# One forget-bias tile per head, and new task costs and transfer model in the planner of a hybrid-attention layer

## The chip, the cores and the metric

The kernel runs on one core of one Trainium2 chip. The metric is the device time of one execution in microseconds; the median over several executions is given. A profiled execution has a time of its own. Engines are called as in the profile: PE (matrix), PEld (its weight loads), DVE (vector), ACT (scalar), POOL (GpSimd) and SP, which here only issues DMAs.

## What is computed

One layer of a streaming encoder, for a prompt of 16 + 1024 rows and, with the same weights, for 32 new rows behind 272 cached ones. Each row of 1024 is normalised (RMSNorm) and projected by one weight into queries, keys and values of two attention groups, 8 forget logits and a gate of 1024 columns. The two groups are four differential heads with a distance bias and eight forgetting heads with a bias from summed log forget gates. Their outputs are concatenated, multiplied by SiLU of the gate, projected by a second weight, added to the input and normalised. New keys, values and log gates are outputs too. Of the reference, the forgetting heads are the part that the change touches:

```python
F = jnp.cumsum(LF, axis=1)
sf = jnp.einsum('bqhe,bkhe->bhqk', qf, Kf).astype(f32) * scale
sf = sf + (Fq_t[:, :, :, None] - Fk_t[:, :, None, :])
sf = jnp.where(kidx[None, :] <= qidx[:, None], sf, NEG)
pf = jax.nn.softmax(sf, axis=-1)
of = jnp.einsum('bhqk,bkhe->bqhe', pf.astype(Vf.dtype), Vf)
```

As the softmax takes out whatever is the same for a whole row, the kernel adds only F of the key minus a constant.

## The kernel before, in words

Everything is written as tasks: an engine, an estimated cost in ns, a function that emits the instructions, a priority (lower comes first), the tasks it depends on and the buffers that it takes and gives back. `Graph.order` (L149) plays the tasks through in time: each engine, when free, takes the ready task of the lowest priority number whose buffers can be had. The order in which tasks begin there is the order in which the instructions are written, and each engine, SP too, runs its own in that order. So the costs, which are set by hand at each `add`, decide the order, but not how long anything takes on the chip. A result is taken to reach another engine after 300 to 500 ns (`HOPS`, L33). Costs come from formulas by columns (`c_mm`, `c_act`, `c_dve`, `c_ts`, `c_pool`, from L266) or from a number. A DMA task holds SP for 480 ns (`dma`, L281), a transpose for 1190; its transfer is played as `moved`, in `order`, which adds 650 ns before, 2.85 ns for each KB and 900 ns behind, with eight in flight at most.

Buffers are rings of so many tiles (`RINGS`) and an `arena` in which room is sought for each use. Rings are counted, but the tile framework hands out a ring's tiles in turn.

The stages of work: the inputs are normalised and transposed into `hT` (`x_tasks`). For each of 8 pairs `p` of columns, `w_tasks` (L611) loads 512 KB of weight into `raw` (L625), takes the largest absolute value on ACT (L627), spreads it over the partitions by a diagonal on POOL (L583) and a matmul on PE (L587), and rounds the weight into two halves of 16 bits; `proj_tasks` multiplies (L827). Pairs 0 to 3 are the differential heads, pairs 4 to 7 two forgetting heads each. `pair_tasks` then makes the attention units: a unit (`unit_tasks`, L1206) is one head with two blocks of 128 queries, `gg` from 0 to 3; for the forgetting pairs head 0 and head 1 take turns for each `gg`. In a unit PE writes scores into one of two PSUM banks `sc` (L1235), DVE adds the bias tile and takes the minimum in one pass (L1249), ACT takes the exponential (L1255), DVE, ACT and POOL split the probabilities into two halves, SP transposes them by DMA from `arena` to `arena` (L1335), and PE multiplies by the values (L1347 to L1349 differential, L1351 and L1352 forgetting). Later pairs' projections and the gates' have high priority numbers and fill PE in between. `out_tasks` (L1607) loads the mixed columns and the gate of one tile of rows (L1719, L1720), multiplies, takes the largest absolute value (L1737), rounds (L1740 on ACT, L1742 on DVE), multiplies by the output weight (L1770), adds the input (L1784) and normalises (L1808), and stores (L1811).

The bias of the forgetting heads: `forget_tasks` makes F for all 8 heads and 1040 rows on 8 partitions, subtracts from it one of four constants (its value at row 16 + 256 `gg`, L1113) and stores the four versions to `G_s` in DRAM. For each pair, `bias_tasks` (L1148) loads its 8 rows (L1177), scales them on POOL (L1180) and stores them to `G_t` (L1184). For each unit it then fetches the first 272 + 256 `gg` columns of one row, broadcast to all 128 partitions, into a tile of the ring `G`, which has two (L1192):

```python
n = 272 + 256 * gg
sp.dma_start(out=loc["t"][:, :n], in_=G_t.rearrange("h n -> (h n)")[None, 8320 * (p - 4) + c:8320 * (p - 4) + c + n]
             .broadcast_to([128, n]))
```

The ring `G` also holds the distance tile of the differential pairs and, at either end, the gains of the two norms.

## Time and profile before

| | |
|---|---|
| time, median of 3 runs (lowest to highest) | 882.83 us (881.67 to 883.38) |
| the profiled execution: its time, its span | 879.12 us, 877.4 us |
| mean granted PE clock of the span | 0.909 |
| busy: PE, DVE, ACT, POOL | 80%, 72%, 57%, 47% |
| DMA: moved in the span, share of the 16 engines of the hardware queue | 119.27 MB, 60.4% |

A busy share is the time in which an engine has an instruction under way. The rest is waiting, and lists of waits say what ended it. A matmul's record also holds its way through the array, so that PE's instructions overlap and a busy PE can still be short of its peak. The clock is given as a share of 2.4 GHz.

### The profile page before, as it was taken

To read this page: it belongs to the slowest core of one execution; us is meant where nothing else is said; L and a number is where in the kernel's file an instruction comes from. 1 tells how busy PE (TensorE), PEld (TensorE's weight loads), DVE (VectorE), ACT (ScalarE), POOL (GpSimd) and SP (SyncE) were. 2 spreads that over 40 slices of the span, in tenths; PEclk is the share of its full clock that TensorE was granted. 3 is DMA by queue.
4 is the path that set the end of the run, shared out by engine and by line. 5 is a ranking of instruction groups with operands and counts; after the bars stand their busy time and mean duration, and the time that the engine had idled before them with its cause. 6 is when DMAs were issued, how large, how long until landed. Compare 5 with 4: busy or idle time off the path is not lost. (4 is left out here: it accounts for less than half of the span.)

```text
span 877.4 us, 14974 instructions
## 1 busy us (share of the span) xinstructions
PE 703.1 (80%) x4967; PEld 456.3 (52%) x4967; DVE 633.0 (72%) x1672; ACT 496.5 (57%) x1136; POOL 414.3 (47%) x602
## 2 busy tenths in 40 slices
PE   4578887987876999899796978689788962888776
PEld 4455554665544576566564755356556542233333
DVE  5976587877766887988985857497797895454443
ACT  5843574666553776676675665377568752242222
POOL 2575233977556866866743654445452244200000
PEclk7679989999998999999998989799999985698899
DMA  8672426454423554554499688467959989753511
GB/s 248 122 147 62 93 54 88 106 94 103 95 65 74 127 102 98 115 117 115 105 194 182 127 168 163 111 144 167 208 123 204 277 204 243 232 173 121 153 63 49
DMA packets 240558, 119.27 MB, mean 136 GB/s; under 512 B 150569, under 2 KB 229745, under 8 KB 240481
## 3 DMA queue, kind: packets, MB, share of 16 engines
q1 hardware_dynamic: 240480, 118.32, 60.4%
q8 instruction: 39, 0.64, 0.3%
q14 instruction: 39, 0.31, 0.1%
HBM read 57.18 MB, written 22.07 MB: 90 GB/s over the span
## 5 line engine op out<-in xcount | busy, mean ns | idle before, releaser
L827 PE MATMUL pj<-hT,Whi 128*128 128x384 f16 (+4 forms) x1328 | 314.7, 321 | 2.0 <-DVE ge L938 1.5
L827 PE MATMUL pj<-hT,Wlo 128*128 128x416 f16 (+4 forms) x664 | 212.6, 320 | 4.4 <-DVE Wlo L648 4.4
L827 PEld LDWEIGHTS <-Whi 128*128 128x128 f16 x1328 | 133.3, 102 | 78.5 <-issue 11.5
L1249 DVE CUSTOM_DVE_ANT_0 arena<-sc,G,stats 128x400 f32<-128x400 f32 (+6 forms) x224 | 129.9, 590 | 43.3 <-PE sc L1235 22.4
L1255 ACT ACTIVATE arena<-arena,stats 128x144 f32<-128x144 f32 (+7 forms) x128 | 99.9, 780 | 38.8 <-DVE stats L1249 31.6
L1235 PE MATMUL sc<-k,q 128*128 128x400 f16 (+6 forms) x448 | 97.1, 317 | 29.4 <-DVE stats L1249 25.7
L583 POOL TENSOR_SCALAR diag<-ident,stats 128x128 bf16<-128x128 f32 x51 | 26.1, 513 | 154.9 <-ACT Wlo L1737 68.5
L827 PEld LDWEIGHTS <-Wlo 128*128 128x128 f16 x664 | 67.6, 102 | 38.1 <-DVE Wlo L648 4.7
L1351 PE MATMUL av<-arena,vn 128*128 128x128 f16 x288 | 43.9, 236 | 45.2 <-DMA arena<-arena 44.7
L1235 PEld LDWEIGHTS <-q 128*128 128x128 f16 x448 | 40.8, 101 | 57.6 <-issue 41.1
L627 ACT ACTIVATE Wlo<-raw 128x1024 bf16<-128x1024 f32 x27 | 28.5, 1055 | 63.8 <-DMA raw<-in_w_in_dram 63.8
L1770 PEld LDWEIGHTS <-Whi 128*128 128x128 f16 (+2 forms) x304 | 30.1, 102 | 58.7 <-issue 16.5
L827 PE MATMUL pj<-hT,Wghi 128*128 128x256 f16 (+2 forms) x240 | 58.2, 326 | 0.0
L1770 PE MATMUL pj<-arena,Whi 128*128 128x512 f16 (+4 forms) x152 | 49.7, 413 | 9.8 <-ACT Whi L1740 7.1
L1352 PEld LDWEIGHTS <-vn 128*128 128x128 f16 x288 | 30.7, 107 | 48.6 <-issue 47.6
L1290 POOL TENSOR_TENSOR arena<-arena 128x16 f16<-128x16 f32 (+7 forms) x56 | 46.5, 853 | 12.4 <-ACT arena L1284 12.1
L1306 DVE SCALAR_TENSOR_TENSOR arena<-arena,stats 128x128 f16<-128x128 f32 (+4 forms) x80 | 49.6, 663 | 2.6 <-ACT arena L1298 2.4
L1323 POOL TENSOR_TENSOR arena<-arena 128x16 f16<-128x16 f32 (+3 forms) x48 | 36.0, 773 | 25.8 <-ACT arena L1317 25.7
L1789 ACT ACTIVATE arena<-arena 128x512 bf16<-128x512 f32 (+3 forms) x19 | 11.5, 603 | 61.4 <-DVE arena L1784 61.4
L1352 PE MATMUL av<-arena,vn 128*128 128x128 f16 x288 | 44.3, 237 | 0.0
L1784 DVE SCALAR_TENSOR_TENSOR arena<-pj,stats,arena 128x512 f32<-128x512 f32 (+3 forms) x19 | 13.7, 721 | 42.3 <-PE pj L1770 38.9
L587 PE MATMUL tr<-diag,onesb 128*128 128x128 bf16 x51 | 11.7, 229 | 36.9 <-POOL diag L583 24.6
(310 smaller groups left out, 1786.7 us busy)
## 6 DMA issues: line engine op xcount, KB each, us to landing
raw<-in_w_in_dram SPq DMA_DIRECT2D x32, 512.0 KB, 7.5
arena<-in_x_prompt_dram SPq DMA_DIRECT2D x16, 512.0 KB, 9.7
raw<-in_w_out_dram SPq DMA_DIRECT2D x16, 512.0 KB, 4.6
k<-k SPq DMA_DIRECT2D x16, 268.0 KB, 3.4
G<-G_t SPq DMA_DIRECT2D x8, 520.0 KB, 4.7
mix_s<-mx SPq DMA_DIRECT2D x32, 128.0 KB, 3.4
arena<-mix_s SPq DMA_DIRECT2D x8, 512.0 KB, 6.3
arena<-gate_s SPq DMA_DIRECT2D x8, 512.0 KB, 6.0
```

The lines of the kernel that those rows point to most:

```text
L583: pool.tensor_scalar(out=loc["d"], in0=ident, scalar1=col_, scalar2=1.0, op0=ALU.mult, op1=ALU.mult)
L627: ta = add("act", c_act(1024), lambda: act.activation(out=loc["lo"].bitcast(BF16), in_=loc["raw"], func=AF.Abs, accum_out=a), prio, [tl], ...
L827: mm(out, (W["hi"], W["hi"], W["lo"])[w][:, k, :], (hTh, hTl, hTh)[w][:, k, c0:c1], start=i == 0, stop=i == 23)
L1235: mm(s[:, :b - a], q, K[p]["t"][:, m, x, a:b], start=x == 0, stop=x == 1 and not mask)
L1249: dve.tensor_tensor_reduce(out=A(ph, nk)[:, a:b], in0=loc["s"][:, :b - a], in1=bl["t"][:, o + a:o + b], scale=Q[p]["tau"], scalar=3e38 if ...
L1255: te = add("act", c_act(nk) + 150, lambda ph=ph, nk=nk, mn=mn, sm=sm: act.activation(out=A(ph, nk), in_=A(ph, nk), func=AF.Exp, scale=-1.0 ...
L1290: (pool if on_pool else dve).tensor_tensor(out=A16(w, o, o + b - a), in0=x[:, a:b], in1=A16(w, h, h + b - a), op=ALU.subtract)
L1306: dve.scalar_tensor_tensor(out=A16(w, o, o + b - a), in0=x[:, a:b], scalar=rk, in1=A16(w, h, h + b - a), op0=ALU.mult, op1=ALU.subtract)
L1323: pool.tensor_tensor(out=A16(w, o, o + b - a), in0=x[:, a:b], in1=A16(w, h, h + b - a), op=ALU.subtract)
L1351: mm(out, vn[:, j, 128 * hd:128 * hd + 128], hi, start=j == 0, stop=False)
L1352: mm(out, vn[:, j, 128 * hd:128 * hd + 128], lw, start=False, stop=False)
L1770: mm(d, a, b, start=k == 0 and i == 0, stop=k == 7 and i == len(ops) - 1)
```

## The change

It has two parts. First, the forget bias: F is taken against one constant only (its value at row 528), stored once per head, scaled once, and fetched once per head of a pair, with all 1040 columns, by one broadcast. Both heads' tiles stay in the ring `G` until their last unit. Second, the planner: nearly every cost is set to another number, a matmul is taken to be slower for a while behind a long pause (`COLD`), the time for a result to reach another engine depends on the engine that gives it (`HOPS`), rings are handed out in turn, and transfers follow one another: a plain DMA's data begins when the one before is through, and a transpose holds SP from shortly before that until its own cost is over and lands 2000 ns later. A part of the output projection is taken to hold only the two weights that it reads.

```diff
-HOPS = [400.0, 300.0], [500.0, 300.0]
+HOPS = {"pe": 220.0, "sp": 100.0, "act": 80.0, "dve": 80.0, "pool": 80.0}
+SLACK = {"pe": 0.0, "act": 0.0, "dve": 0.0, "pool": 0.0, "sp": 0.0}
+COLD = 3400.0
+TRANSPOSED = 2000.0
+LANDED = 1600.0
...
-MARGIN = 1.1
...
-                if self.free[h.ring] < 1:
+                if self.slots[h.ring][self.turn[h.ring]]:
                     break
-                self.free[h.ring] -= 1
+                h.at = self.turn[h.ring]
+                self.slots[h.ring][h.at] = True
+                self.turn[h.ring] = (h.at + 1) % self.free[h.ring]
...
-                    d.ready = max(d.ready, now + (0.0 if d.eng == t.eng else HOPS[d.eng == "pe"][d.prio > 10400]))
+                    d.ready = max(d.ready, now + (0.0 if d.eng == t.eng else HOPS[t.eng] + SLACK[d.eng]))
...
-                        busy[e] = now + t.cost
+                        cost = t.cost
+                        if e == "pe":
+                            if now > last + COLD:
+                                slow = COLD
+                            cost += min(cost, slow)
+                            slow = max(0.0, slow - cost + t.cost)
+                            last = now + cost
+                        busy[e] = now + cost
                         done = busy[e]
-                        if e == "sp":
-                            moved = max(done + 650.0, moved) + t.move
-                            done = moved + 900.0
-                            flight = (flight + [done] * t.n)[-8:]
-                            if len(flight) == 8:
-                                busy[e] = max(busy[e], flight[0])
+                        if t.dma:
+                            if t.block:
+                                busy[e] = done = moved = max(now, moved - 300.0) + t.cost
+                                done += TRANSPOSED
+                            else:
+                                busy[e] = max(busy[e], moved - 4000.0)
+                                moved = max(busy[e] + 300.0, moved) + t.move
+                                done = moved + LANDED
...
-        return k * max(107.0, 0.417 * n)
+        return k * max(56.0, 2.5 + 0.417 * n)
     def c_act(n, k=1):
-        return MARGIN * k * (75.0 + 0.84 * n)
+        return k * (165.0 + 0.85 * n)
     def c_dve(n, k=1):
-        return MARGIN * k * (65.0 + 1.05 * n)
+        return k * (165.0 + 1.08 * n)
     def c_ts(n):
-        return MARGIN * (100.0 + 1.1 * n)
+        return 240.0 + 1.05 * n
     def c_pool(n, k=1):
-        return MARGIN * k * (100.0 + 2.2 * n)
-    def dma(fn, prio, deps=(), acq=(), use=(), kb=128, n=1, spare=(), cost=480.0):
-        t = add("sp", cost * n, fn, prio, deps, acq, use, 2.85 * kb, spare)
+        return k * (160.0 + 2.2 * n)
+    def dma(fn, prio, deps=(), acq=(), use=(), kb=128, n=1, spare=(), cost=440.0, move=4.5, block=False):
+        t = add("sp", cost * n, fn, prio, deps, acq, use, move * kb, spare)
         t.n = n
+        t.dma = True
+        t.block = block
...
-    G_s = dr.tile([NH, 4 * 1040], F32, tag="G_s", name="G_s")
-    G_t = dr.tile([NH, 4 * 1040], F32, tag="G_t", name="G_t")
+    G_s = dr.tile([NH, 1040], F32, tag="G_s", name="G_s")
+    G_t = dr.tile([NH, 1040], F32, tag="G_t", name="G_t")
...
-        t1 = add("act", cost + 330, f1, prio, deps, [], use)
-        return r, t1, add("dve", 530, f2, prio, [t1, by and by[1]])
+        t1 = add("act", cost + 420, f1, prio, deps, [], use)
+        return r, t1, add("dve", 1170, f2, prio, [t1, by and by[1]])
...
-                    kb=5 * w, cost=1190.0)
+                    kb=5 * w, cost=2640.0, block=True)
...
-        td = add("pool", 260, fd, prio, list(deps) + [cn["id"]], [dh])
-        return loc, th, add("pe", 110, f, prio, [td, cn["one"]], [th], [dh])
+        td = add("pool", 370, fd, prio, list(deps) + [cn["id"]], [dh])
+        return loc, th, add("pe", 60, f, prio, [td, cn["one"]], [th], [dh])
...
-        tl = dma(fl, prio, [], [rh, wh], kb=512)
+        tl = dma(fl, prio, [], [rh, wh], kb=512, move=10.0)
...
-        t4 = add("pool", 1500, f4, prio, [t3], [], [sh, vh])
+        t4 = add("pool", 3000, f4, prio, [t3], [], [sh, vh])
...
-        for gg in range(4):
-            n = 1040
-            gh = Hold("arena", n)
-            def fg(gg=gg, n=n, gh=gh):
-                F = A(Fh, 1040, NH)
-                b = 16 + 256 * gg
-                dve.tensor_scalar(out=A(gh, n, NH), in0=F[:, :n], scalar1=F[:, b:b + 1], scalar2=None, op0=ALU.subtract)
-            tg = add("dve", 65 + 0.6 * n, fg, prio, carry, [gh], [Fh])
-            G_done[gg] = dma(lambda gg=gg, n=n, gh=gh: sp.dma_start(
-                out=G_s[:, 1040 * gg:1040 * gg + n], in_=A(gh, n, NH)), prio, [tg], [], [gh])
+        gh = Hold("arena", 1040)
+        def fg():
+            F = A(Fh, 1040, NH)
+            dve.tensor_scalar(out=A(gh, 1040, NH), in0=F, scalar1=F[:, 528:529], scalar2=None, op0=ALU.subtract)
+        tg = add("dve", 65 + 0.6 * 1040, fg, prio, carry, [gh], [Fh])
+        G_done["p"] = dma(lambda: sp.dma_start(out=G_s, in_=A(gh, 1040, NH)), prio, [tg], [], [gh])
...
-    def bias_tasks(p, hd, gg, prio, G_done):
+    def bias_tasks(p, hd, prio, G_done):
...
-        n = 272 + 256 * gg
-        if ("G", p) not in samp:
+        if hd == 0:
             gh = Hold("arena", 1040)
             a = 2 * (p - 4)
             def fl():
-                sp.dma_start(out=A(gh, 1040, 8), in_=G_s[a:a + 2].rearrange("h (g n) -> (h g) n", g=4))
+                sp.dma_start(out=A(gh, 1040, 2), in_=G_s[a:a + 2])
             def fm():
-                pool.tensor_scalar(out=A(gh, 1040, 8), in0=A(gh, 1040, 8), scalar1=Q[p]["inv"][:8], scalar2=1.0,
+                pool.tensor_scalar(out=A(gh, 1040, 2), in0=A(gh, 1040, 2), scalar1=Q[p]["inv"][:2], scalar2=1.0,
                                    op0=ALU.mult, op1=ALU.mult)
             def fo():
-                sp.dma_start(out=G_t[a:a + 2].rearrange("h (g n) -> (h g) n", g=4), in_=A(gh, 1040, 8))
-            t = dma(fl, prio - 50, [G_done[x] for x in range(4)] + [Q[p]["t_tau"]], [gh], kb=33)
+                sp.dma_start(out=G_t[a:a + 2], in_=A(gh, 1040, 2))
+            t = dma(fl, prio - 50, [G_done["p"], Q[p]["t_tau"]], [gh], kb=8)
             t = add("pool", 100 + 1.1 * 1040, fm, prio - 50, [t], [], [gh])
-            samp["G", p] = dma(fo, prio - 50, [t], [], [gh], kb=33)
+            samp["G", p] = dma(fo, prio - 50, [t], [], [gh], kb=8)
+        c = 2 * (p - 4) + hd
         def f():
             loc["t"] = T([128, 1040], F32, "G", RINGS["G"])
-            c = 1040 * (4 * hd + gg)
-            sp.dma_start(out=loc["t"][:, :n], in_=G_t.rearrange("h n -> (h n)")[None, 8320 * (p - 4) + c:8320 * (p - 4) + c + n]
-                         .broadcast_to([128, n]))
-        cn["bias"] = dma(f, prio, [samp["G", p], cn["bias"]], [h], kb=n / 2)
+            sp.dma_start(out=loc["t"], in_=G_t[c:c + 1].broadcast_to([128, 1040]))
+        cn["bias"] = dma(f, prio, [samp["G", p], cn["bias"]], [h], kb=520)
...
-                     prio, [tl], [z], [w], kb=20 * nt, cost=1190.0)
+                     prio, [tl], [z], [w], kb=20 * nt, cost=1100.0 + 40.0 * nt, block=True)
...
-                             [ph] if part == 0 else [], [wh] + wholds + ([ph] if part else []))
+                             [ph] if part == 0 else [], [wh] + wholds[2 * part:2 * part + 2] + ([ph] if part else []))
...
-        dist = None
+        dist = {}
         for u, (hd, gg) in enumerate(units):
-            if p >= 4 or u == 0:
-                dist = bias_tasks(p, hd, gg, base + u - 1, G_done)
+            if hd not in dist:
+                dist[hd] = bias_tasks(p, hd, base + u - 1, G_done)
             if hd == 0:
                 av = {}
-            unit_tasks(p, hd, gg, base + u, dist, av)
+            unit_tasks(p, hd, gg, base + u, dist[hd], av)
```

Left out are further costs of single tasks, changed in the same way, among them those of the sample rows' tasks and of the rounding in the units.

## Rows read from the trace of the kernel before

**Rows 1.** Head of the page: the span.

```profile
span 877.4 us, 14974 instructions
PE 703.1 (80%) x4967; PEld 456.3 (52%) x4967; DVE 633.0 (72%) x1672; ACT 496.5 (57%) x1136; POOL 414.3 (47%) x602
```

**Rows 2.** Busy by stage: stretch, its length, each engine's busy us (instructions), clock, DMA.

```profile
100.00:360.00 260.00, 221.81 (x1621) 148.34 (x1619) 199.94 (x552) 160.49 (x380) 167.56 (x225) 0.95 0.46 92
360.00:720.00 360.00, 300.04 (x2391) 207.35 (x2391) 282.55 (x810) 238.73 (x550) 178.92 (x285) 0.96 0.76 162
720.00:877.00 157.00, 114.12 (x513) 50.49 (x512) 76.81 (x161) 42.70 (x95) 20.10 (x21) 0.82 0.51 148
```

**Rows 3.** PE's waits, whole span: who waited for whom, us, times, longest.

```profile
PE av L1351 <- DMA arena<-arena: 44.7, 21, 8.7
PE sc L1235 <- DVE stats L1249: 25.7, 29, 3.0
PE tr L587 <- POOL diag L583: 24.6, 9, 5.6
...
PE tr L587 <- ACT stg L712: 8.7, 3, 5.9
...
PE av L1347 <- DMA arena<-arena: 1.8, 2, 1.1
```

**Rows 4.** Line L1335, 100 to 370 us: ns on SP (min/median/max), then landing.

```profile
L1335 SPq DMA_TRANSPOSE arena<-arena x25: 1177/1401/5860, 109.6 to 366.1; - x25
...
DMA to landing us min/median/max: 2.6/3.8/5.8
```

**Rows 5.** The same line, 370 to 740 us.

```profile
L1335 SPq DMA_TRANSPOSE arena<-arena x71: 1177/1760/6361, 371.9 to 731.2; - x71
...
DMA to landing us min/median/max: 3.3/4.6/13.0
```

**Rows 6.** Timeline of SP, 545 to 554 us: start, us, what.

```profile
545.69 1.03 SPq L625 DMA_DIRECT2D raw<-in_w_in_dram  x1
546.89 6.36 SPq L1335 DMA_TRANSPOSE arena<-arena  x1
```

**Rows 7.** DMA queue and issues, 370 to 735 us: KB each, median us to landing.

```profile
q1 hardware_dynamic: 129574, 59.36, 76.2%
...
raw<-in_w_in_dram SPq DMA_DIRECT2D x12, 512.0 KB, 7.4
G<-G_t SPq DMA_DIRECT2D x8, 520.0 KB, 4.7
...
G<-G_t SPq DMA_DIRECT2D x8, 136.0 KB, 3.4
```

**Rows 8.** Longest waits of all engines, whole span.

```profile
ACT Wlo L627 <- DMA raw<-in_w_in_dram: 63.8, 21, 8.2
```

**Rows 9.** Line L1192: ns on SP (min/median/max), first and last start.

```profile
L1192 SPq DMA_DIRECT2D G<-G_t x32: 319/392/1590, 371.0 to 701.4; - x32
```

**Rows 10.** Line L1113, the subtractions of the forget task.

```profile
L1113 DVE TENSOR_SCALAR arena<-arena x4: 743/744/749, 133.7 to 135.7; 8x1040 f32<-8x1040 f32 x4
```

**Rows 11.** PE's waits, 720 to 878 us.

```profile
PE pj L1770 <- ACT Whi L1740: 7.1, 4, 1.9
PE pj L1770 <- DVE Wlo L1742: 6.9, 4, 2.8
PE tr L587 <- POOL diag L583: 5.6, 1, 5.6
PE tr L587 <- DVE stats L600: 3.4, 4, 1.0
PE pj L1770 <- DVE Whi L1742: 2.7, 1, 2.7
```

**Rows 12.** Timeline of all engines, 814 to 822 us.

```profile
817.22 2.17 ACT L1740 ACTIVATE Whi<-arena,stats 128x1024 f16<-128x1024 f32 x2
...
820.91 0.61 PE L1770 MATMUL pj<-arena,Wlo 128*128 128x512 f16 x1 [1.47 <-DVE Wlo L1742]
```

More of the change, by code (lines that the diff above doesn't have):

```diff
@@ L69, in __init__ @@
         self.n = 1
+        self.dma = eng == "sp"
+        self.block = False
         self.holds = list(acq) + list(use)
@@ L96, in __init__ @@
         self.free = dict(rings)
+        self.slots = {r: [False] * n for r, n in rings.items()}
+        self.turn = dict.fromkeys(rings, 0)
         self.arena = arena
@@ L137, in _take @@
         ok = len(got) == len(t.acq) + len(spare)
-        for h in got[len(t.acq):] if ok else got:
+        for h in got[len(t.acq):] if ok else got[::-1]:
             self._give(h)
+            if h.ring != "arena":
+                self.turn[h.ring] = h.at
         return ok
@@ L146, in _give @@
         else:
-            self.free[h.ring] += 1
+            self.slots[h.ring][h.at] = False
     def order(self):
@@ L161, in order @@
         n = 0
-        now = moved = 0.0
-        flight = []
+        now = 0.0
+        last = slow = 0.0
+        moved = 0.0
         while events or later:
@@ L964, in fq @@
                     pool.tensor_copy(out=qz[2][o:o + 64, 32 * m:32 * m + 32], in_=q[o:o + 64])
-            Q[p]["z"] = add("pool", 950, fq, prio, [Q[p]["sample"], cn["c"], samp.get(("score", p - 1))], [], [Q[p]["qh"]])
+            Q[p]["z"] = add("pool", 870, fq, prio, [Q[p]["sample"], cn["c"], samp.get(("score", p - 1))], [], [Q[p]["qh"]])
             inv, tau = stat(), stat()
@@ L1241, in unit_tasks @@
                         deps.append(ts)
-                    ts = add("pe", c_mm(b - a, 2) + (56 if mask else 0), fs, prio + 0.5, deps,
+                    ts = add("pe", c_mm(b - a, 2) + (66 if mask else 0), fs, prio + 0.5, deps,
                              [sh] + ([ph] if ci == 0 else []), [Q[p]["hold"][0 if i < 2 else 1 if i < 5 else 2], K[p]["hold"]] + ([ph] if ci else []),
@@ L1251, in fr @@
                                                  op1=ALU.min, accum_out=new)
-                    tr_ = add("dve", c_dve(b - a), fr, prio + 0.5, [ts, bt] + ([tr_] if ci else []), [], [sh, ph, bh])
+                    tr_ = add("dve", c_dve(b - a) + 60, fr, prio + 0.5, [ts, bt] + ([tr_] if ci else []), [], [sh, ph, bh])
                     mn = new
                 sm, r, rk = stat(), stat(), stat()
-                te = add("act", c_act(nk) + 150, lambda ph=ph, nk=nk, mn=mn, sm=sm: act.activation(
+                te = add("act", c_act(nk) + 125, lambda ph=ph, nk=nk, mn=mn, sm=sm: act.activation(
                     out=A(ph, nk), in_=A(ph, nk), func=AF.Exp, scale=-1.0, bias=mn, accum_out=sm), prio + 0.4, [tr_], [], [ph])
@@ L1326, in unit_tasks @@
                 on_pool = on_pool and not full
-                th = add("pool" if on_pool else "act", 390 + 1.1 * nb if on_pool else c_act(nb) + 180, fh, prio + 0.2, [t], [w], [P[m]], spare=[nb + 64])
+                th = add("pool" if on_pool else "act", 430 + 0.93 * nb if on_pool else c_act(nb) + 220, fh, prio + 0.2, [t], [w], [P[m]], spare=[nb + 64])
             on_pool = on_pool if p < 4 else full
-            tl = add("pool" if on_pool else "dve", c_pool(nb) + 130 if on_pool else c_dve(nb) + 85, fl, prio + 0.2, [th], [], [w, P[m]])
+            tl = add("pool" if on_pool else "dve", c_pool(nb) + 170 if on_pool else c_dve(nb) + 150, fl, prio + 0.2, [th], [], [w, P[m]])
             z = Hold("arena", nb + 64)
```

54 lines of the change are left out of this document (27 added, 27 removed).

## The prediction

> **What bounds the kernel now.** I read the head of the page, then the busy times by stage, then who PE waited for, and last the SP queue.
>
> No engine fills the span: PE, the longest, is busy for 703.1 of 877.4 us [rows 1]. The stages tell more [rows 2]. From 100 to 360 us (the four differential pairs) PE is busy for 221.81 of 260 us, 85.3%. From 360 to 720 us (the four forgetting pairs) it is 300.04 of 360 us, 83.3%, with DVE at 282.55 (78.5%). From 720 us on, mostly the output projection, it is 114.12 of 157 us. So PE sets the pace, and what can be won is its idle time: the reader should look at what ended it.
>
> The list of PE's waits [rows 3] has one outstanding line: the attention-times-value matmuls of the forgetting heads (L1351) waited 44.7 us for `arena<-arena`, the DMA transposes of the probabilities; the differential heads (L1347), which use the same transposes, 1.8 us. Next come the score matmuls, which waited 25.7 us for DVE to free one of the two `sc` banks (the change adds no bank, so I leave this line as it is), and the little matmul that spreads a scale (L587): 24.6 us behind POOL's diagonal, 8.7 us behind ACT.
>
> Why transposes are late shows on the SP queue. In the differential stretch a transpose holds SP for 1.401 us (median) and lands after 3.8 [rows 4]; in the forgetting stretch for 1.760, up to 6.361, and lands after 4.6, up to 13.0 [rows 5]. At 546.89 us one behind a weight load issued 1.2 us before it held SP for 6.36 us [rows 6]. The planner of before gives every transpose 1.19 us on SP, whatever is in flight. The same holds for weights: by its formula a 512 KB load lands 480 + 650 + 2.85 x 512 + 900 ns = 3.5 us after it starts, the trace says 7.4 [rows 7]. As every engine runs the written order, ACT stands at the absolute maximum of a weight that isn't there (63.8 us, 21 times [rows 8]), and the scale, POOL's diagonal and PE's L587 are late behind it.
>
> **The change part by part.** (a) *One tile per head.* Before, 32 broadcasts fetch 128 x (272 + 256 `gg`) floats, 8 for each `gg`: by the code 8 x (136 + 264 + 392 + 520) KB = 10.5 MB. After, 8 of 520 KB = 4.2 MB. Of the 59.36 MB that the hardware queue moved from 370 to 735 us [rows 7], 6.3 MB or 11% go. On SP 24 issues of 0.392 us (median) go [rows 9]: 9.4 us of a queue on which compute waits only through late transfers, so their gain is counted in (c), not twice. In the forget task three subtractions of 0.744 us on DVE [rows 10] and three stores go, early, with projections of other pairs as cover; I cost them at nothing, and at 2.2 us gained if the gate chain were uncovered. The scaling on POOL keeps its length, since its rows only shrink from 8 to 2 partitions. The reduction L1249 reads the same columns for each chunk. What is added: a pair's first tile now is 520 KB, which lands after 4.7 us, where 136 KB took 3.4 [rows 7]: 1.3 us at each of 4 pair starts, 5.2 us if nothing covers it. The cover is the pair before, whose units go on meanwhile; I take 0. And a tile is held to the end of its pair: see the rivals.
>
> (b) *Costs and hops.* The order on every engine is rewritten, so no single wait can be followed over. What I can judge is where old figures missed the trace. A weight load now is planned as 440 + 300 + 10 x 512 + 1600 ns = 7.46 us, against 7.4 measured [rows 7]. Upper bound of the gain: PE's waits on L587 outside the output stage, 24.6 - 5.6 + 8.7 = 27.7 us [rows 3, 11]; lower bound 0, as each such wait may be replaced by the next instruction's. I take 8, nearer to nothing: part of it lies in the first 100 us, where weights and the inputs compete for the queue and no order has them earlier.
>
> (c) *Transposes in series.* A transpose now starts only when what was issued before it has nearly gone (`moved - 300`), blocks SP for 1100 + 40 nt ns and lands 2.0 us later: 3.8 us for the longest, nt = 17, on an empty queue. The planner so puts the matmuls later, and has loads not cut in ahead of an urgent transpose. Lower bound: the forgetting stage reaches the PE share of the differential stage, where these waits are nearly absent: 300.04 / 0.853 = 351.7 us instead of 360, a gain of 8.3. Upper bound: a wait per transpose like there, 1.8 us over 25 [rows 3, 4], or 5.1 us over 71 [rows 5]: a gain of 39.6. Between lies DVE: at 78.5% it has room, but if the stage shrank by 39.6 it would be at 88%, which it reaches in no stage now. I take 20, a little under the middle.
>
> (d) *The output stage.* PE's waits from 720 us on, without the transposes: 7.1 + 6.9 + 2.7 + 5.6 + 3.4 = 25.7 us [rows 11]. They recur between token tiles: at 817.22 us ACT begins to round two tiles' activations, after the tile before has run out on PE, and full matmul work resumes at 820.91 [rows 12]. The priority of the older tile in the planner, which is not changed, makes PE take its matmuls before the next tile's spread, so better durations help only where loads come earlier. Upper bound 25.7, lower bound 0; I take 5.
>
> On this the Trainium skill has a rule against the change (Perfetto Trace Analysis, Optimization Strategy): the same gap repeating on the engine that should be saturated can mean that there isn't enough SBUF or PSUM for the next tile. The change adds no buffer, so by this rule (d) gives 0, the sum is 28 and the time 855 us; the recurring gaps of [rows 12] agree with it, and no run here separates it from the order.
>
> Sum: 0 + 8 + 20 + 5 = 33 us. The profiled execution took 879.12 us (span 877.4 and 1.7 around it), 3.7 below the median of 882.83. So 879.1 - 33 + 3.7 = 850 us.
>
> **The rivals.** *The tile held too long (slower).* `G` has two buffers. Before, a unit's tile loads while the other head's unit runs. After, the next pair's tile can load only when the last reduction of the same head has read its buffer. A unit lasts (701.4 - 371.0) / 31 = 10.7 us [rows 9]; the load takes 0.4 us of issue and 4.7 of landing [rows 7, 9], and 6.4 more behind a transpose at its worst [rows 5]: 11.5 us. The point is whether the other head's last unit is still to come when the tile comes free: then it covers, as the priorities (head 0 before head 1 in each group) suggest. If both heads end together, the scores stop for up to 11.5 us at each of 3 pair boundaries, 11.5 to 34.5 us as projections fill one, two or none of them. With (c) at its lower bound and the rest at 0 that is 886 to 909 us; I take 893. Against it: PE has projections of later pairs and gates queued in that stage. I give slower endings 0.19 in all, this one most of it.
>
> *The wait moves (no change).* PE no longer stands before L1351 but before L1235, since DVE hands out banks at its own pace (25.7 us now [rows 3]); (c) falls to 8.3, the pair starts cost their 5.2, (b) and (d) give nothing: 880 us, chance 0.07. For it speaks DVE's share, against it that PE's waits are longer at transposes than at banks.
>
> *The plan fits well.* (c) at 39.6, (b) at 15, (d) at 10: 818 us, chance 0.14. It needs everything to go right at once, and the series model still knows nothing of the landings of 13.0 us [rows 5]. That the change doesn't do what it says can't be ruled out either: if the new constants are as far off as the old ones in the forgetting stage, the order is merely another one, and the time ends in the two cases before this one.
>
> **How the numbers follow.** The forecast, 835 to 874 us, has 0.60; the good plan 0.14; no change 0.07; slower 0.19. A measurement of this kernel can tell about 0.2%, 1.8 us, from no change, so faster 0.74, same 0.07, slower 0.19. The forecast's upper end is (c) at 8.3 with all else 0. The range for 8 in 10 reaches into both sides: down to 822, which takes in part of the good plan, and up to 891, nearly to the middle of the slower case; some 0.08 lies below and 0.1 above.
>
> **What would show it.** The list of issues has 8 `G<-G_t` of 520 KB and none of the smaller forms; about 53 MB move in the forgetting stage. L1351's wait on `arena<-arena` falls from 44.7 to some 20 us, and the forgetting stage from 360 to about 340 us. ACT's wait on `raw` falls clearly under 63.8 us. The output stage is shorter by little, with its gaps still there. I am wrong if the transposes' wait stays at 40 us or more, if PE or DVE stands before L1249 for a tile at pair boundaries (11 us each), or if the span moves for a stage that I gave nothing: the first 100 us, or the differential pairs.

## The result and the profile after

The change takes the time from 883.11 to **857.85 us** (855.37 to 860.0), a ratio of 0.9715 with a 95% interval of 0.9682 to 0.9747. The forecast was 850, the range 822 to 891. The profiled execution took 855.37 us, its span is 853.6.

The head of the page after, against [rows 1]; PE's busy time is the same to 0.8 us, so 23.0 of the 23.8 us of span are idle time of PE, as the prediction had looked for it.

```profile
span 853.6 us, 14870 instructions
PE 702.3 (82%) x4967; PEld 455.0 (53%) x4967; DVE 627.1 (73%) x1669; ACT 496.8 (58%) x1136; POOL 409.1 (48%) x602
```

To see where they went, I set two kinds of events side by side: the weight loads of the forgetting heads' attention-times-value matmuls, and those of the output projection (first and last start). Before:

```profile
L1351 PEld LDWEIGHTS <-vn x288: 95/98/153, 433.2 to 737.6; 128*128 128x128 f16 x144
...
L1770 PEld LDWEIGHTS <-Whi x304: 92/98/152, 746.9 to 870.3; 128*128 128x128 f16 x136, 128*32 128x32 f16 x14, 128*64 128x64 f16 x2
```

After:

```profile
L1373 PEld LDWEIGHTS <-vn x288: 95/98/153, 433.1 to 705.0; 128*128 128x128 f16 x144
...
L1792 PEld LDWEIGHTS <-Whi x304: 92/98/154, 724.2 to 847.0; 128*128 128x128 f16 x136, 128*32 128x32 f16 x14, 128*64 128x64 f16 x2
```

The forgetting heads begin at 433 us in both. They take 304.4 us before and 271.9 after: **32.5 us gained**. Then PE stands between the last of them and the first output matmul, 9.3 us before and 19.2 after: **9.9 us lost**. From there to the end it is 130.5 and 129.4 us. 32.5 + 0.1 - 9.9 + 1.1 = 23.8.

The equal start hides a part of the gain: PE has done more by then. By stretch (us, busy us of PE, PEld, DVE, ACT, POOL; granted clock, DMA share, GB/s), before:

```profile
0.00:433.00 433.00, 356.02 (x2582) 244.17 (x2583) 337.53 (x872) 266.74 (x620) 265.61 (x372) 0.92 0.50 107
433.00:737.70 304.70, 239.86 (x1935) 168.08 (x1934) 229.10 (x658) 190.96 (x430) 136.94 (x216) 0.92 0.83 176
```

After:

```profile
0.00:433.00 433.00, 364.36 (x2628) 247.68 (x2629) 341.60 (x878) 269.11 (x623) 260.74 (x372) 0.93 0.50 108
433.00:705.00 272.00, 231.78 (x1889) 163.22 (x1888) 214.16 (x645) 188.61 (x426) 131.19 (x212) 0.91 0.78 161
```

PE's idle time falls by 8.3 us up to 433 us and by 24.6 us in the forgetting heads' stretch; the work done ahead makes up the rest of the 32.5.

PE's waits up to the end of the attention (0 to 697 us), against [rows 3]:

```profile
PE sc L1257 <- DVE stats L1271: 29.4, 35, 3.7
PE av L1373 <- DMA arena<-arena: 15.8, 7, 3.9
PE tr L614 <- POOL diag L610: 12.6, 5, 7.2
...
PE av L1369 <- DMA arena<-arena: 3.4, 3, 1.9
```

The wait for transposes, 44.7 us before, is 15.8 here and 19.3 over the whole span; the one for the scale's diagonal, 19.0 us outside the output stage before, is 12.6, and ACT's line of 8.7 is 1.3. The wait for a score bank, which the change doesn't touch, is 29.4 (25.7).

The transposes on SP in the forgetting stretch (370 to 740 us; ns on SP, then landing), against [rows 5]:

```profile
L1357 SPq DMA_TRANSPOSE arena<-arena x72: 1177/1484/5486, 369.8 to 698.6; - x72
...
DMA to landing us min/median/max: 2.3/4.1/6.3
```

No landing is over 6.3 us, where the worst was 13.0. The longest waits of ACT hold the line of [rows 8] in its new form, 18.6 instead of 63.8 us:

```profile
ACT Wlo L654 <- DMA raw<-in_w_in_dram: 18.6, 5, 4.9
```

The broadcasts are eight (ns on SP; no instruction waits for one of them by name), and the hardware queue moves 111.53 MB in the span where it moved 118.32:

```profile
L1215 SPq DMA_DIRECT2D G<-G_t x8: 320/682/1363, 396.0 to 637.9; - x8
...
q1 hardware_dynamic: 236880, 111.53, 58.1%
```

The chain that ended last, from 697 to 727 us (start, us, what), shows the hole of 19.2 us:

```profile
699.21 2.30 SPq L1357
701.51 0.05 issue
701.56 0.74 SPq L1395
702.31 0.04 issue
702.35 0.44 SPq L1649
702.79 0.04 issue
702.84 4.93 DMA raw<-in_w_out_dram
...
707.82 1.29 DVE arena L1712
709.13 3.70 DMA raw<-in_w_out_dram
712.83 0.08 issue
712.91 1.13 POOL arena L1708
714.07 1.29 DVE arena L1712
715.38 0.33 SPq L1649
715.71 0.05 issue
715.77 0.03 issue
715.80 0.39 SPq L1741
716.18 0.05 issue
716.24 3.88 DMA arena<-gate_s
```

The output weight is read a second time and rounded (L1649, L1708, L1712) in the same SP order as the loads of the mixed columns and the gate (L1741, L1742), and ahead of them: a transpose holds SP for 2.3 us, the weight's next tile waits until DVE has freed a buffer, and only at 715.8 us is the first mixed tile asked for. That is 10.8 us behind the last attention matmul; before, it was 2.0 us ahead of it (735.6 and 737.6). In the code of both, this request also waits for four loads of the second reading (`wloads`). The issues of the mixed tiles, before and after (first and last start):

```profile
L1719 SPq DMA_DIRECT2D arena<-mix_s x9: 377/384/2414, 735.6 to 822.1; - x9
...
L1741 SPq DMA_DIRECT2D arena<-mix_s x9: 377/377/1955, 715.8 to 797.1; - x9
```

PE's wait for the diagonal is then 16.5 us long. In the middle of the hole (columns as above):

```profile
700.00:720.00 20.00, 2.97 (x32) 2.69 (x32) 6.23 (x8) 0.68 (x1) 6.53 (x5) 0.56 0.77 218
```

PE is busy for 2.97 of 20 us there, and its clock is down to 0.56, so for most of it at 1.2 GHz, the lower of its two levels. The gaps between the output's token tiles are nearly as they were: in PE's waits from 720 us on the two lines that led [rows 11] read 7.1 (7.1) and 5.2 (6.9) us.

```profile
PE pj L1792 <- ACT Whi L1762: 7.1, 4, 1.9
PE pj L1792 <- DVE Wlo L1764: 5.2, 4, 1.6
```

### The profile page after: what moved, and what is told of

It is laid out like the page before. It is cut to its first block, busy times and chain, and to the rows that moved or that the text cites. A ratio compares the mean times of both kernels' runs of the same rounds, so it can differ in the third digit from the quotient of the medians.

```text
span 853.6 us, 14870 instructions
## 1 busy us (share of the span) xinstructions
PE 702.3 (82%) x4967; PEld 455.0 (53%) x4967; DVE 627.1 (73%) x1669; ACT 496.8 (58%) x1136; POOL 409.1 (48%) x602
## 3 DMA queue, kind: packets, MB, share of 16 engines
q1 hardware_dynamic: 236880, 111.53, 58.1%
## 5 line engine op out<-in xcount | busy, mean ns | idle before, releaser
L854 PE MATMUL pj<-hT,Whi 128*128 128x416 f16 (+4 forms) x1328 | 309.1, 318 | 4.5 <-DMA hT<-arena 2.3
L854 PEld LDWEIGHTS <-Whi 128*128 128x128 f16 x1328 | 131.4, 100 | 78.2 <-issue 16.7
L1271 DVE CUSTOM_DVE_ANT_0 arena<-sc,G,stats 128x400 f32<-128x400 f32 (+7 forms) x224 | 129.7, 590 | 35.0 <-PE sc L1257 20.5
L1257 PE MATMUL sc<-k,q 128*128 128x400 f16 (+7 forms) x448 | 102.3, 327 | 32.8 <-DVE stats L1271 29.4
L1277 ACT ACTIVATE arena<-arena,stats 128x528 f32<-128x528 f32 (+7 forms) x128 | 99.9, 781 | 43.9 <-DVE stats L1271 41.7
L854 PEld LDWEIGHTS <-Wlo 128*128 128x128 f16 x664 | 66.5, 100 | 33.4 <-issue 2.8
L1373 PE MATMUL av<-arena,vn 128*128 128x128 f16 x288 | 44.8, 239 | 19.3 <-DMA arena<-arena 19.3
L1312 POOL TENSOR_TENSOR arena<-arena 128x16 f16<-128x16 f32 (+7 forms) x56 | 48.9, 898 | 8.7 <-ACT arena L1306 8.5
L880 POOL TENSOR_SCALAR k<-zT 64x416 f16<-64x416 f32 (+4 forms) x50 | 31.1, 622 | 27.1 <-ACT zT L872 25.0
L1345 POOL TENSOR_TENSOR arena<-arena 128x16 f16<-128x16 f32 (+3 forms) x48 | 33.9, 729 | 20.0 <-ACT arena L1339 17.6
L1374 PEld LDWEIGHTS <-vn 128*128 128x128 f16 x288 | 31.1, 108 | 19.3 <-issue 17.6
L614 PE MATMUL tr<-diag,onesb 128*128 128x128 bf16 x51 | 11.7, 230 | 34.2 <-POOL diag L610 29.5
L1323 POOL TENSOR_SCALAR arena<-arena,stats 128x128 f16<-128x128 f32 (+2 forms) x32 | 21.2, 672 | 38.2 <-DVE stats L1281 12.9
```

Of the source, the lines that this page charges most:

```text
L854: mm(out, (W["hi"], W["hi"], W["lo"])[w][:, k, :], (hTh, hTl, hTh)[w][:, k, c0:c1], start=i == 0, stop=i == 23)
L880: pool.tensor_scalar(out=K[p]["t"][a:b, m, 0, c0:c1], in0=z()[a:b], scalar1=1.0, scalar2=1.0, op0=ALU.mult, op1=ALU.mult)
L1257: mm(s[:, :b - a], q, K[p]["t"][:, m, x, a:b], start=x == 0, stop=x == 1 and not mask)
L1271: dve.tensor_tensor_reduce(out=A(ph, nk)[:, a:b], in0=loc["s"][:, :b - a], in1=bl["t"][:, o + a:o + b], scale=Q[p]["tau"], scalar=3e38 if ...
L1277: te = add("act", c_act(nk) + 125, lambda ph=ph, nk=nk, mn=mn, sm=sm: act.activation(out=A(ph, nk), in_=A(ph, nk), func=AF.Exp, scale=-1.0 ...
L1312: (pool if on_pool else dve).tensor_tensor(out=A16(w, o, o + b - a), in0=x[:, a:b], in1=A16(w, h, h + b - a), op=ALU.subtract)
```

## The experiments

The question was which part of the change earns the gain: the bias tiles, the transfer model, or the new costs and hops. Twelve kernels ran; all compute the whole layer. Ratios are to executions of the kernel before that were timed with each (their medians: 880.8 to 883.1 us). "Waits" are PE's for transposes (both kinds of head) and ACT's for `raw` (`Wlo` and `Wglo`), from the profile of each.

| kernel | time, us | ratio (95%) | PE for transposes | ACT for `raw` |
|---|---|---|---|---|
| before | 883.11 | | 46.5 | 82.2 |
| the change | 857.85 | 0.9715 (0.9682 to 0.9747) | 22.7 | 18.8 |
| bias part alone | 872.12 | 0.9875 (0.9851 to 0.9898) | 49.7 | 81.4 |
| all but the bias part | 890.84 | 1.0105 (1.0071 to 1.0139) | 23.1 | 25.7 |
| all but the transfer model | 927.21 | 1.0483 (1.0448 to 1.0518) | 68.1 | 103.6 |
| bias part and transfer model | 848.41 | 0.9596 (0.9559 to 0.9633) | 12.7 | 5.0 |
| same, new plain transfers alone | **816.77** | 0.9249 (0.9198 to 0.9301) | 22.3 | 17.0 |
| same, blocking transposes alone | 854.59 | 0.9691 (0.9646 to 0.9735) | 27.2 | 78.6 |

**Bias part alone.** The kernel before with the new `forget_tasks` and `bias_tasks`; costs, hops and transfers are the old ones.

```diff
-        cn["bias"] = dma(f, prio, [samp["G", p], cn["bias"]], [h], kb=n / 2)
+        cn["bias"] = dma(f, prio, [samp["G", p], cn["bias"]], [h], kb=520)
...
```

> The kernel before with the bias part of the change alone: one tile per head, 8 broadcasts instead of 32, old costs, old transfer model. Theory (the planner's figures give the gain, the saved traffic little): 868 to 888 us, L1351-type waits on transposes still over 30 us in all. Rival (the 6.3 MB less in the forgetting stage give the gain): at most 865 us, with those waits near the 19 us of the changed kernel. Rival (a tile held to the end of the pair costs a wait at pair boundaries): over 890 us, DVE or PE before the score reduction for a G tile.

It took 872.12 us. PE's waits of this kernel (the two lines for transposes):

```profile
PE av L1346 <- DMA arena<-arena: 37.1, 17, 7.3
...
PE av L1342 <- DMA arena<-arena: 12.6, 4, 7.0
```

The forgetting heads' line falls by 7.6 us, the differential heads' line rises by 10.8, yet the time falls by 11. The part is worth something by itself, but the transposes are as late as before: it doesn't cure them.

**All but the bias part.** The new planner with the old 32 broadcasts (the same lines, the other way).

> The changed kernel with the old bias part put back: 32 broadcasts of growing size, new costs and new transfer model. Theory (the planner's figures give the gain): 852 to 868 us, waits of the forgetting matmuls on transposes under 30 us. Rival (the traffic gives it): 872 us or more, those waits near 44 us.

890.84 us, 1% slower than before. The time is the rival's, the waits are the theory's: 23.1 and 25.7 us, near those of the whole change (22.7 and 18.8). So these two waits don't tell the time. The head of its page:

```profile
PE 719.6 (81%) x4967; PEld 466.4 (52%) x4967; DVE 636.8 (72%) x1672; ACT 498.4 (56%) x1136; POOL 414.7 (47%) x602
```

Of the 35.2 us of span between the two kernels 17.3 are PE's own busy time, 719.6 us against 702.3 for the same 4967 matmuls, at a mean granted clock of 0.893 against 0.907. Why the clock is lower wasn't tried. The new planner by itself gains nothing, and the two parts don't add: 11 us of the bias part over the old planner, 33 over the new. The 22 us between these are about what a mere shuffle of the order can do (below).

**All but the transfer model.** New bias and new costs, hops and rings, with the old transfers:

```diff
-                            if t.block:
-                                busy[e] = done = moved = max(now, moved - 300.0) + t.cost
-                                done += TRANSPOSED
-                            else:
-                                busy[e] = max(busy[e], moved - 4000.0)
-                                moved = max(busy[e] + 300.0, moved) + t.move
-                                done = moved + LANDED
+                            moved = max(done + 650.0, moved) + t.move
+                            done = moved + 900.0
+                            flight = (flight + [done] * t.n)[-8:]
+                            if len(flight) == 8:
+                                busy[e] = max(busy[e], flight[0])
...
-                    kb=5 * w, cost=2640.0, block=True)
+                    kb=5 * w, cost=1190.0)
...
-        tl = dma(fl, prio, [], [rh, wh], kb=512, move=10.0)
+        tl = dma(fl, prio, [], [rh, wh], kb=512)
...
-                     prio, [tl], [z], [w], kb=20 * nt, cost=1100.0 + 40.0 * nt, block=True)
+                     prio, [tl], [z], [w], kb=20 * nt, cost=1190.0)
```

> The changed kernel with the old model of transfers put back (480 ns of issue, 2.85 ns per KB, 900 ns behind, transposes of 1190 ns that don't block), all new costs of compute, the new hops and the new bias part kept. Theory (the serial transfers are what moved the transposes' waits): those waits go back to 35 us or more and ACT's waits on weight loads to 50 us or more, time 868 to 885 us. Rival (measured durations and hops give the gain): 852 to 864 us, waits on transposes under 25 us.

"Serial" needs a word. Plain transfers stand one behind the other in both planners: both take `moved` from the transfer before. New are the figures (4.5 ns for each KB instead of 2.85, 10 for weights; 1600 ns behind instead of 900) and that SP stands when more than 4000 ns of transfers lie ahead, not when eight are in flight. Where the description of the change and the expectations say "serial", this set is what was switched; its members weren't tried one by one. A transpose that blocks SP is new altogether.

927.21 us, the slowest of all, 42 above the theory's range. Its waits:

```profile
PE av L1372 <- DMA arena<-arena: 49.3, 24, 5.8
...
PE av L1368 <- DMA arena<-arena: 18.8, 11, 7.3
...
ACT Wlo L653 <- DMA raw<-in_w_in_dram: 93.4, 25, 9.1
```

Without the model both waits are above those of before. The heads' first matmul comes at 474.0 us instead of 433: the loss begins in the pairs ahead of it.

**Bias part and transfer model.** The first kernel with the change's transfers; compute costs, `HOPS`, `MARGIN` and ring counting stay old.

```diff
...
-        tl = dma(fl, prio, [], [rh, wh], kb=512)
+        tl = dma(fl, prio, [], [rh, wh], kb=512, move=10.0)
...
-                     prio, [tl], [z], [w], kb=20 * nt, cost=1190.0)
+                     prio, [tl], [z], [w], kb=20 * nt, cost=1100.0 + 40.0 * nt, block=True)
...
```

> The kernel before with the new bias part and the new model of transfers (serial, blocking transposes, 10 ns per KB for weights), but the old costs of compute and the old hops. Theory (serial transfers give the gain): 855 to 868 us, waits on transposes under 25 us, ACT's waits on weights under 35 us. Rival (durations give it): 872 us or more. Both together, with neither alone, would be 865 to 880 us here and in the run with old transfers.

848.41 us, 9 under the whole change and below the theory's range. The four kernels with the new bias make a square: with old costs, the transfer model takes 872.1 to 848.4 (24 us), with new costs 927.2 to 857.9 (69 us). The new costs, with hops and rings, take 872.1 to 927.2 with old transfers and 848.4 to 857.9 with new ones: they don't help in either row. PE's waits of this kernel:

```profile
PE tr L594 <- POOL diag L590: 25.9, 5, 16.6
...
PE av L1353 <- DMA arena<-arena: 12.0, 8, 2.6
```

The line for transposes is at its second lowest of all the runs, and the hole ahead of the output stage (16.6 us in one wait) is there as in the change.

**Old hops.** The change with `HOPS` as before:

```diff
-HOPS = {"pe": 220.0, "sp": 100.0, "act": 80.0, "dve": 80.0, "pool": 80.0}
+HOPS = [400.0, 300.0], [500.0, 300.0]
...
```

> The changed kernel with the old hops (300 to 500 ns from one engine to another), all else as changed. Theory (the new hops of 80 to 220 ns are what makes the new compute figures worse than the old ones: a plan with no slack makes engines stand at instructions whose input is a little late): 840 to 852 us, as good as the run with new transfers and old costs (848.4). Rival (the new durations themselves, or rings handed out in turn, are what hurts): 855 to 870 us.

848.91 us (0.9638, 0.9577 to 0.9699), 9 us under the change, with 29.6 us of waits for transposes (no less than the change's) and a hole of 9.4 us (709.7 to 719.1). Against the change the hole is 9.8 us shorter and the stage behind it 3.0, while the attention ends 4.7 later. Whether the short hops cause this or another order would do the same, this run can't say.

**Is it the order alone?** Any edit of a cost gives another order. Two controls change the factor on the cost formulas of ACT, DVE and POOL by 2%, which no theory of transfers cares for: `MARGIN` from 1.1 to 1.08, in the kernel before and in the bias part with the transfer model. In the second one, as in the two halves below, a part of the output projection holds its two weights only, as in the change; in the kernel of 848.41 us that line leaves the order as it was.

```diff
-MARGIN = 1.1
+MARGIN = 1.08
```

> A control: the kernel before with its compute costs scaled by 1.08 instead of 1.10, which says nothing new of the chip and only shuffles the order. Theory (what the parts did is more than a shuffle): 878 to 888 us, within 0.6% of before. Rival (any other order scatters by several per cent, so that single parts can't be told apart): more than 10 us away from 883.

> A second control: new bias, new transfers, and the old compute costs scaled by 1.08 instead of 1.10; the order is merely shuffled. Theory (a shuffle is worth under 1% with the new transfers too, so the 9 us between 848 and 858 us belong to hops and costs): 843 to 855 us. Rival (with the new transfers orders scatter by more, and the 9 us may be a shuffle): outside of that.

The first took 882.77 us (1.0028, 0.9994 to 1.0061): nothing. The second took 829.42 us (0.9404, 0.9361 to 0.9447): 19 us less than without the edit, its waits nearly the same (10.3 for the forgetting heads' transposes, 8.6 for `raw`, the hole 19.1 us), its forgetting heads from 399.2 to 678.7 us instead of 418.8 to 694.9. So the rival holds in part: a mere shuffle moved one kernel by nothing and the other by 19 us. Two controls bound that poorly, so I call a difference between two orders shown only where it is well over 20 us: the 24 us of the model over the old costs are near that (43 with the shuffled order), its 69 us over the new ones are more than three times the larger shuffle.

**The hole.** One reason for it could be that the output weight's scale is known late. `last_q` makes its first reading wait for the last pair's queries; here it waits for those of the pair before, in the change and in the bias part with the transfer model:

```diff
-            last_q = Q[p]["lo"][0]
+            if p < 7:
+                last_q = Q[p]["lo"][0]
```

> The changed kernel, where the first reading of the output weight (for its largest absolute value) may begin with pair 6's queries instead of pair 7's. Theory (the hole of PE at 700 to 720 us of the changed kernel stands because the scale of the output weight is known only at 700 us, and its second reading starts behind it): the scale is known before 680 us, PE's hole shrinks by 8 to 15 us, time 842 to 852 us. Rival (the hole comes from room in the arena, held by the last attention units, or from the transfers themselves): 855 to 862 us, with the second reading still behind 695 us; or slower, if the early loads take the buffers of the input weights.

> The same edit on the kernel with new bias, new transfers and old compute costs (848.4 us). Theory: 832 to 842 us. Rival (room or transfers): 845 to 852 us, or slower if the early loads take buffers of the input weights.

865.05 us (0.9822, 0.9761 to 0.9883) and 845.47 us (0.9613, 0.9538 to 0.9688): one slower, one the same. The gap between attention and output goes from 19.2 to 7.2 us and from 19.3 to 0.6, but the attention itself ends 20.3 and 17.5 us later (725.3 and 712.4). The hole is so only moved. That the early readings take their transfers from the attention would fit, but isn't shown: the transposes' waits rise from 22.7 to 33.4 us in the first kernel and are 12.7 and 12.5 in the second, and an edit's shuffle can be as large. In the second kernel part of the hole can be seen earlier:

```profile
660.00:670.00 10.00, 1.12 (x9) 0.96 (x9) 2.79 (x7) 3.88 (x8) 3.33 (x3) 0.52 1.04 216
```

PE is busy for 1.12 of 10 us with the DMA share at 1.04. A late scale alone isn't the cause: in the first kernel ACT is through the first reading by 681.6 us instead of 695.9, yet the second reading begins at 712.3 instead of 702.4. What goes with the hole in all fourteen kernels is when SP asks for the first mixed tile: the first output matmul begins 7.7 to 11.7 us after it. That request comes 10.7 to 10.8 us behind the last attention matmul in the three kernels with a hole of 19 us, 2.8 behind it in the fastest kernel (below), and ahead of it in the other ten. What holds it back (the loads ahead of it on SP, a full queue, buffers that aren't free, or `wloads`) wasn't tried one by one.

**Which half of the transfer model.** From the bias part with the transfer model (848.41 us), first only plain transfers are the new ones, and a transpose is one of them, with 1190 ns on SP; then only transposes block, and plain transfers are the old ones:

```diff
-                    kb=5 * w, cost=2640.0, block=True)
+                    kb=5 * w, cost=1190.0, move=2.85)
...
-                     prio, [tl], [z], [w], kb=20 * nt, cost=1100.0 + 40.0 * nt, block=True)
+                     prio, [tl], [z], [w], kb=20 * nt, cost=1190.0, move=2.85)
```

> The run with new bias, new transfers and old compute costs (848.4 us), with the transposes taken back to a plain transfer of 1190 ns on SP that blocks nothing; plain transfers stay serial, weights at 10 ns per KB. Theory (the blocking transpose in the plan is the larger part, since the forgetting matmuls' waits on transposes fell most): 858 to 872 us, these waits back over 30 us, ACT's waits on weights still under 35 us. Rival (the slower weights in the plan are the larger part): 846 to 856 us.

```diff
-                                busy[e] = max(busy[e], moved - 4000.0)
-                                moved = max(busy[e] + 300.0, moved) + t.move
-                                done = moved + LANDED
+                                moved = max(done + 650.0, moved) + t.move
+                                done = moved + 900.0
+                                flight = (flight + [done] * t.n)[-8:]
+                                if len(flight) == 8:
+                                    busy[e] = max(busy[e], flight[0])
...
-        tl = dma(fl, prio, [], [rh, wh], kb=512, move=10.0)
+        tl = dma(fl, prio, [], [rh, wh], kb=512)
```

> The other half: new bias, old compute costs, transposes that block in the plan, but plain transfers as before (2.85 ns per KB, eight in flight, weights too). Theory: 850 to 862 us, waits on transposes under 25 us, ACT's waits on weights 45 us or more. Rival (weights are the larger part): 862 to 875 us.

816.77 us, below both ranges, and 854.59, as its theory had it. Of the 872.12 us of the bias part alone, new plain transfers take 55, blocking transposes 17.5, which is within the scatter of orders. The longest waits of the first:

```profile
PE av L1353 <- DMA arena<-arena: 21.5, 14, 7.9
...
ACT Wlo L634 <- DMA raw<-in_w_in_dram: 12.9, 4, 4.8
```

And of the second:

```profile
PE av L1356 <- DMA arena<-arena: 20.8, 11, 5.3
...
ACT Wlo L637 <- DMA raw<-in_w_in_dram: 58.8, 21, 7.2
```

Either half brings the transposes' wait down to 21 us. Only the half with new plain transfers brings the weights in time, and that line sorts all the kernels by planner, though not by time: with new plain transfers ACT waits 5 to 29 us on `Wlo` (the change and seven others), without them 58 to 93 (before and five others). The 816.77 us kernel from 100 to 360 us (columns as above):

```profile
100.00:360.00 260.00, 235.27 (x1782) 159.31 (x1783) 227.83 (x620) 180.61 (x436) 182.33 (x248) 0.99 0.51 102
```

PE is busy for 235.27 of 260 us here (90%; [rows 2] has 221.81), but so it nearly is with both halves (233.85). Its forgetting heads start at 409.3 us instead of 433 and take 259.8 us; the hole is 10.5. Against both halves they start 9.5 us earlier and take 16.3 less, the hole is 8.8 shorter and what follows 6.4 longer. That plain transfers alone beat both halves together by 32 us isn't shown to be their doing: with both halves in the shuffled order (829.42 us) only 12.7 are left. It is the fastest version found, 7.5% under before.

**The bias part: bytes or tasks?** The kernel with the bias part alone, in the very same order, and 24 broadcasts more (136, 264 or 392 KB, from `G_t` into DRAM that nobody reads), issued at the start of the later units:

```diff
+                        if p >= 4 and gg and bi == 0 and ci == 0:
+                            w = 16 + 256 * gg
+                            d = dr.tile([128, w], F32, tag=f"xt{p}{hd}{gg}", name=f"xt{p}{hd}{gg}")
+                            c = 2 * (p - 4) + hd
+                            sp.dma_start(out=d, in_=G_t[c:c + 1, :w].broadcast_to([128, w]))
```

> The bias part alone (872.1 us), in the same order of all other instructions, with 24 more broadcasts of 136, 264 and 392 KB into DRAM that nobody reads, one at the start of each later unit of a forgetting head: the old bytes and the old issues on SP, without the old order and without waits for a tile. Theory (the bias part's 11 us come from 24 fewer broadcasts before the transposes on the queue): 878 to 888 us, waits of the forgetting matmuls on transposes longer by 5 us or more. Rival (they come from the order, or from tiles that no longer have to land for each unit): 869 to 876 us.

880.06 us (875.22 to 887.73; 0.9979, 0.9942 to 1.0016). The queue moves 118.02 MB, as before, and 8 of the 11 us are gone again. As the order is the same, scatter of orders has no part in this: what the bias part earns is mostly its saved transfers and their issues, not the tasks it leaves out. Its profiled run, at the low end of its spread, shows the transposes later by a little, 3.4 us for the forgetting heads where 5 or more were expected:

```profile
PE av L1351 <- DMA arena<-arena: 40.5, 18, 8.2
...
PE av L1347 <- DMA arena<-arena: 14.9, 6, 7.7
```

## Why the prediction was right, and where not

**(a) One tile per head, 0 us.** Its kind was right (bytes and issues, felt through late transfers), its booking wasn't: "their gain is counted in (c), not twice" made it a part of the planner's gain, but it stands by itself with 11 us over the old order, of which 8 come back with the bytes. The slow rival, a tile held too long, didn't come: neither PE nor DVE waited for a `G` tile.

**(b) and (c), 8 and 20 us.** Together 28, and up to the last attention matmul the kernel gained 737.6 - 705.0 = 32.6 us. That 8.3 us of PE's idle time went before 433 us, with PE busy for 10 us more in the differential pairs' stretch (231.88 us from 100 to 360 us; [rows 2] has 221.81), is one of my own signs of being wrong: I had given that stage nothing. And the parts look sized the wrong way round. I gave the weights 8 us, "nearer to nothing", and put the transposes first; the halves of the model say 55 us for the new plain transfers and 17.5 for blocking transposes, each with some 20 us of scatter, and they don't add up (24 together). The rows were there: 21 waits of ACT on `raw` [rows 8] and a load that took 7.4 us where the planner had 3.5 [rows 7]. I took them for PE's waits on the spread scale only; but the model of a weight also tells the planner when the queue is taken, which would fit the transposes that come in time with it (21.5 us of waits with transposes still taken as ordinary). "In series" was the wrong word for what is new in (c): the old planner had its transfers in series too, at lower figures.

That the change's costs and hops would help was never shown as a step of its own, and in these orders they don't: in the square they are worth nothing with new transfers (9 us worse, within the scatter) and cost 55 us with the old. The planner as a whole, to which I gave all 33 us, gains only together with the new bias; alone it took 890.84 us. Why is open.

**(d) The output stage, -5 us: the step that failed.** From the last attention matmul to the end it took 139.8 us before and takes 148.6: 8.8 us worse where 5 better were forecast, which is 13.8 of the sum's 33. "Better durations help only where loads come earlier" was right, but I took it that they come no later. I priced the gaps within the stage and not the wait at its start: the first mixed tile was asked for 2.0 us before the last attention matmul and now is 10.8 us behind it, and PE stands for 19.2 us instead of 9.3. That isn't bound to follow from an attention that ends 33 us earlier: in the 816.77 us kernel it ends at 669.1 us, with a hole of 10.5. The recurring gaps, on which the Trainium skill's rule bore (Perfetto Trace Analysis, Optimization Strategy: the same gap repeating on the engine that should be full can mean too little SBUF or PSUM), are 7.1 and 5.2 us, before 7.1 and 6.9; by that rule alone (d) was 0 and the time 855 us, nearer to what came, though the hole that made the difference isn't one of these gaps. That buffers are the reason was not tried.

So the sum was 32.6 - 8.8 = 23.8 us instead of 33, and the median lies 2.5 us above the profiled run instead of 3.7. That the time fell into the forecast is in part luck: (b) and (c) were 4.6 too low and (d) 13.8 too high, and a shuffle of 19 us is half as wide as the forecast (835 to 874 us). Of the signs, the transposes' line (19.3, "some 20"), ACT's on `raw` (18.6) and the eight broadcasts came as said; the forgetting heads' stretch shrank by 32.5 us where some 20 were said. The 53 MB forecast for 370 to 735 us didn't come: 58.98 MB, since the output stage's own loads now begin inside that stretch; over the whole span it is 6.8 MB less.

## What to carry to other kernels

Where a hand-written planner sets the order, compare its formula for each kind of transfer with the landing times in the trace first, the largest plain loads before anything else: here, with the new bias, new figures for transfers took 24 to 69 us off, and new durations for all compute tasks gained nothing. Before an edit of such a planner is credited with a few per cent, run a control that only shuffles the order; here one moved the time by 19 us. And when a stage gets shorter, look at when the first load of the next one is asked for: here that came 10.8 us behind the last matmul instead of 2.0 ahead of it, and a third of what the attention had gained went there.

## What the runs showed of the hardware

A load of 512 KB isn't a load of 512 KB: in the same stretch (370 to 735 us) those from `w_in`, whose columns lie in runs of 512 bytes, land in 7.4 us [rows 7] and those from `w_out`, whole rows of 4 KB, in 4.5 (median; DMA issues of the kernel before). The fastest of each in the whole run took 5.7 and 3.5.

```profile
raw<-in_w_out_dram SPq DMA_DIRECT2D x13, 512.0 KB, 4.5
```

The Trainium skill names a fixed overhead of each packet and a fixed amount of metadata for each DMA operation (DMA: Bandwidth & Descriptors, Why small descriptors are slow), and puts the first at 27% for 256 bytes. The direction agrees; but these loads differ by 64% at 512 bytes, so by that figure the cost is at most a part of it, and what else was in flight isn't the same for both.

And a transpose of the probabilities never held SP for less than 1.18 us, but for up to 5.5 in the change and 12.7 in the kernel without the bias part. One that follows a weight load at 1.2 us held it for 6.36 [rows 6]; that what was issued before it sets this time fits, but wasn't tried.
